# Gates and half of z as column pairs with seven products for eight, ahead of the groups

## The chip, the cores and the metric

One core of a Trainium2 chip. The metric is the device time of one execution in microseconds (us), the median of several runs.

## The reference

One step of a hybrid decoder layer on T = 1032 tokens (1024 new positions and 8 single decode tokens), width 1024, all in float32:

```python
xn = rms_norm(x)
z, xbc, dt, u, gate_a, gate_b = split(xn @ w_in)     # 2048, 4096, 32, 1024, 1024, 1024 columns
x, B, C = silu(causal_conv(xbc))                     # 8 groups: B and C of 128, x of 256 columns
y_a = rms_norm((ssd_scan(x, dt, B, C) + d * x) * silu(z))
y_b = mix(trailing means of u over 2, 4, 8, 16 positions, minus u)
merged = sigmoid(gate_a) * (y_a @ w_branch_a) + sigmoid(gate_b) * (y_b @ w_branch_b)
h = x_in + rms_norm(merged @ w_out)
out = h + rms_norm((silu(g) * up) @ w_ffn_out)       # g, up = rms_norm(h) @ w_ffn_in
```

The scan runs in chunks of 128 positions, its state carried from chunk to chunk.

## The kernel before

Values lie with 128 channels on the partitions and tokens along the row. Each float32 operand is split in two parts, a rounded high part (ACT copies) and the rest (DVE subtracts), and each product is three matmuls: high x high, high x low, low x high (`mm3`, L229). Columns of a weight come in blocks of 128; a block of the input projection reads the eight row blocks `xh[k]`, `xl[k]` in three token thirds of 344 (`in_unit`, L317): 3 x 8 x 3 = 72 matmuls. `load_w` (L172) takes weights in the order of a fixed plan, splitting one ahead, two buffers each.

The stages: input norm; pooling branch (`pool_proj`, `pool_group`, `pool_mix`, four pool groups, the mix of one beside the columns of the next); eight groups (`group_proj`, L615: conv columns B, C, x0, x1 with their four-tap conv on DVE, then two z blocks with SiLU), each beside the scan of the group before (`ssd`, L646, 18 steps, one for each token third); then 16 gate blocks (`gates`, L619) beside the last scan, with the mixer's norm and the splits of the first branch quarter at set places (L629 to L636); six branch quarters (L852), each splitting the next quarter's operands; output projection, norms, FFN in, FFN out.

FFN in (`prep`, `product`) takes a gate and an up column block against two token halves as a 2 x 2 block product with seven products for eight: weight sums and operand sums are made on DVE, each product is four row blocks x three matmuls on 258 columns, twice for the two token halves. A unit there is one column pair against 516 or 1032 tokens.

In `rp` lie 36 rows of 1060 floats, shared by all. Instructions are put in each engine's queue by a scheduler that lets an instruction go ahead of earlier code if its inputs and its buffers are there; on the chip each queue then runs in order. Two weight buffers, four banks `pj`, two `T`, one `S`, one `y` in PSUM.

## Time and profile before

| | |
|---|---|
| time, median of 3 runs | 2148.2 us (2147.57 to 2150.14) |
| the profiled execution, first to last instruction | 2146.5 us |
| busy: PE, DVE, ACT, POOL | 2091.0, 1361.0, 791.1, 406.9 us |
| moved by DMA | 243.74 MB, 114 GB/s on the mean |
| groups 2 to 5, 441 to 789 us | 348 us |
| end of the groups to the first branch quarter | 831.6 to 1032.6 us |

The profile is of one execution; no device time of its own is listed beside its span, so the span stands against the median of the runs. PE's busy time is modelled from pipelined matmuls: where PE is at its pace is read from the distance of like events. DVE, ACT and POOL times are measured, and neighbours on one engine overlap a little.

### The profile page before, as it was taken

Reading aid. Unit: us, or ns where it says so; the run is one execution under the profiler, and the core shown is the slowest. Engines: PE = TensorE matmul, PEld = TensorE weight load, DVE = VectorE, ACT = ScalarE, POOL = GpSimd, SP = SyncE. Lnnn points to the kernel's source line nnn. Section 1 sums busy time; section 2 is a strip of 40 time slices with the busy share of each in tenths; the row PEclk is TensorE's granted clock in tenths of the full one; section 3 lists DMA queues with packets and bytes.
Section 4 is the critical chain, followed back from the end, with each engine's and each line's share of the span. In section 5 each row is a group of like instructions: output and inputs, shape, how many; then the busy total and the mean of one; then the engine's idle time right before and its main releaser. Section 6 shows DMA issues by size and latency. Waiting matters only on the chain.

```text
span 2146.5 us, 36509 instructions
## 1 busy us (share of the span) xinstructions
PE 2091.0 (97%) x14722; PEld 2055.9 (96%) x14722; DVE 1361.0 (63%) x2283; ACT 791.1 (37%) x1530; POOL 406.9 (19%) x407
## 2 busy tenths in 40 slices
PE   6999999999999999999999999989999999999997
PEld 5999999999999999999999999989999999999997
DVE  7665578677787776422155775679777666654436
ACT  5443344444444444233331024445333233351112
POOL 3100234424434243210100001352000000000004
PEclk9999999999999999999999999989999999999998
DMA  3332343334434334433343444234322222252133
GB/s 126 97 112 72 100 125 125 124 105 142 139 99 127 116 128 149 137 118 136 117 150 101 145 135 151 101 101 142 96 95 90 72 78 90 99 188 69 40 101 107
DMA packets 121961, 243.74 MB, mean 114 GB/s; under 512 B 24896, under 2 KB 62912, under 8 KB 121792
## 3 DMA queue, kind: packets, MB, share of 16 engines
q1 hardware_dynamic: 121360, 241.12, 35.0%
q8 instruction: 116, 1.90, 0.4%
q14 instruction: 53, 0.43, 0.1%
q10 hardware_dynamic: 432, 0.28, 0.0%
HBM read 189.38 MB, written 51.98 MB: 112 GB/s over the span
## 4 chain that ended last, share of the span: by engine, by line
PE 71%; DVE 8%; ACT 2%; DMA 2%; issue 2%; POOL 2%; SPq 0%; DVEq 0%; ACTq 0%; POOLq 0%
PE pj L230 20%; PE pj L232 20%; PE pj L231 20%; DVE S L595 2%; DMA E<-s_ac 1%; PE y L709 1%; PE y L230 1%; PE y L231 1%; PE y L232 1%; DVE S L597 1%; PE T L230 1%; PE T L232 1%; PE T L231 1%; PE S L231 1%; PE S L232 1%
## 5 line engine op out<-in xcount | busy, mean ns | idle before, releaser
L230 PE MATMUL pj<-xh,wh 128*128 128x344 f32 x1728 | 563.3, 327 | 2.4 <-ACT xh L299 2.4
L231 PE MATMUL pj<-xl,wh 128*128 128x344 f32 x1728 | 553.0, 320 | 0.1
L232 PE MATMUL pj<-xh,wl 128*128 128x344 f32 x1728 | 552.8, 320 | 0.0
L230 PEld LDWEIGHTS pj<-xh,wh 128*128 128x128 f32 x1728 | 324.9, 188 | 14.3 <-issue 11.0
L231 PEld LDWEIGHTS pj<-xl,wh 128*128 128x128 f32 x1728 | 325.5, 188 | 1.4 <-DVE xl L300 0.8
L232 PEld LDWEIGHTS pj<-xh,wl 128*128 128x128 f32 x1728 | 325.2, 188 | 0.0
L167 DVE TENSOR_TENSOR wl<-wr,wh 128x1024 fp32r<-128x1024 f32 (+1 forms) x125 | 170.4, 1364 | 210.0 <-ACT wh L166 210.0
L166 ACT CAST wh<-wr 128x1024 fp32r<-128x1024 f32 x142 | 146.6, 1033 | 363.4 <-PE pj L231 335.5
L917 POOL TENSOR_TENSOR ssacc<-ssacc,sq 128x258 f32<-128x258 f32 (+3 forms) x41 | 43.7, 1072 | 923.8 <-ACT sq L916 917.7
L230 PE MATMUL pj<-qh,wh 128*128 128x344 f32 (+1 forms) x608 | 189.7, 312 | 0.0
L231 PE MATMUL pj<-ql,wh 128*128 128x344 f32 (+1 forms) x608 | 189.7, 312 | 0.0
L232 PE MATMUL pj<-qh,wl 128*128 128x344 f32 (+1 forms) x608 | 189.6, 312 | 0.0
L231 PE MATMUL pj<-al,wh 128*128 128x344 f32 (+2 forms) x528 | 168.9, 320 | 0.0
L232 PE MATMUL pj<-ah,wl 128*128 128x344 f32 (+2 forms) x528 | 168.8, 320 | 0.0
L230 PE MATMUL pj<-ah,wh 128*128 128x344 f32 (+2 forms) x528 | 168.8, 320 | 0.0
L683 ACT ACTIVATE E<-E,acT 128x128 f32<-128x128 f32 x256 | 83.9, 393 | 214.8 <-DMA E<-s_ac 198.1
L595 DVE SCALAR_TENSOR_TENSOR S<-U,hcw,S 128x1056 f32<-128x1056 f32 x96 | 137.3, 1430 | 3.0 <-ACT S L593 2.9
L1172 DVE TENSOR_TENSOR acc<-acc,pj 128x344 f32<-128x344 f32 (+2 forms) x120 | 60.8, 510 | 98.0 <-PE pj L232 97.9
L231 PEld LDWEIGHTS pj<-ql,wh 128*128 128x128 f32 x608 | 114.4, 188 | 0.0
L232 PEld LDWEIGHTS pj<-qh,wl 128*128 128x128 f32 x608 | 114.4, 188 | 0.0
L230 PEld LDWEIGHTS pj<-qh,wh 128*128 128x128 f32 x608 | 114.3, 188 | 0.0
L232 PEld LDWEIGHTS pj<-ah,wl 128*128 128x128 f32 x528 | 99.3, 188 | 0.0
(351 smaller groups left out, 4898.1 us busy)
## 6 DMA issues: line engine op xcount, KB each, us to landing
wr<-wi SPq DMA_DIRECT2D x72, 512.0 KB, 4.3
E<-s_ac SPq DMA_DIRECT2D x64, 256.0 KB, 4.0
wr<-wfi SPq DMA_DIRECT2D x30, 512.0 KB, 3.6
s_act<-wk SPq DMA_DIRECT2D x44, 258.0 KB, 2.0
ar<-s_act SPq DMA_DIRECT2D x22, 516.0 KB, 4.7
wu<-wfi SPq DMA_DIRECT2D x22, 512.0 KB, 3.7
wr<-wfo SPq DMA_DIRECT2D x20, 512.0 KB, 3.7
s_y<-Y SPq DMA_DIRECT2D x16, 516.0 KB, 3.8
```

The lines of the kernel that those rows point to most:

```text
L166: act.copy(out=wh, in_=raw)
L167: eng.tensor_tensor(out=wl, in0=raw, in1=wh, op=ALU.subtract)
L230: pe.matmul(out, wh, xh, start=start, stop=False)
L231: pe.matmul(out, wh, xl, start=False, stop=False)
L232: return pe.matmul(out, wl, xh, start=False, stop=stop)
L595: dve.scalar_tensor_tensor(out=S[:, :CW], in0=U[:, k:k + CW], scalar=tap(k), in1=S[:, :CW], op0=ALU.mult, op1=ALU.add)
L597: dve.scalar_tensor_tensor(out=S[:, :CW], in0=U[:, 0:CW], scalar=1.0, in1=S[:, :CW], op0=ALU.add, op1=ALU.mult)
L683: act.activation(out=E[:, h], in_=E[:, h], func=AF.Relu, scale=-1.0, bias=acT[:, c, 4 * g + h:4 * g + h + 1])
L709: pe.matmul(o, xdt[:, h, :], E[:, h, :], start=True, stop=True)
L917: eng.tensor_tensor(out=sacc[:, sl], in0=sacc[:, sl], in1=q, op=ALU.add)
L1172: dve.tensor_tensor(out=acc[ob][:, sl], in0=acc[ob][:, sl], in1=pt, op=ALU.add)
```

## The change

The input columns of both gates and of z in groups 0, 2, 4 and 6 (`ZS`) are no longer projected block by block. A new stage between the pooling branch and the groups makes them as twelve column pairs (`PAIRS`). Each pair is a 2 x 2 block product over row halves, columns and token halves with seven products for eight (`product1`): two accumulate two by two in PSUM, the rest is added on DVE at the eviction. `t_sums` makes the operand sums in the normed rows, `t_split` splits them; T1 is laid over the upper token half of `xh` and `xl` 0 to 3, whose own halves are saved to DRAM before and loaded again by `restore`. Weight sums and splits are made three items ahead (`prep1`, `RING`). A finished pair gets its tanh (z its whole SiLU) and goes to DRAM (`s_ga`, `s_gb`, `s_z`); the z rows come back at step 15 of the scan. The fourth pooling group and its mix move into this stage. PSUM is laid out anew for it and again after it.

Groups 0, 2, 4, 6 then hold four blocks, the others six. The scan beside a group takes 1.5 or 1.12 steps for each token third, and the scan of a group without z starts two steps late. The last scan runs beside the first branch quarter; that quarter's operands are loaded and split right before, the second quarter's later, and the mixer's norm moves into branch quarter 2. The split of the first quarter's weights alternates between DVE and POOL.

```diff
+H = T // 2
+ZS = (0, 2, 4, 6)
+PAIRS = "ga0 ga1 z0 ga2 z2 ga3 z4 gb0 z6 gb1 gb2 gb3".split()
+MIXES = {2: 3}
+RING = 3
+TAILS = (1, 4)
+PROD1 = ("B11", "T2", "B21", "T3", "T1", "T4", "B22")
...
-        n += 1
-        if side is not None and n % every == 0:
+def interleave(main, side, steps):
+    for n, _ in enumerate(main):
+        for _ in range(int((n + 1) * steps) - int(n * steps) if side is not None else 0):
             if next(side, StopIteration) is StopIteration:
                 side = None
+                break
     if side is not None:
         for _ in side:
             pass
...
+        for n, name in enumerate(PAIRS):
+            for i in range(2):
+                want(("pr", name, i), wi[pair_base(name) + i], raw="xp" if i else "wr")
+            if n in MIXES:
+                want(("pr", "m", MIXES[n]), wpool[MIXES[n]], 512, raw="wr")
         for g in range(G):
-            for i, blk in enumerate((WB + g, WC + g, WX + 2 * g, WX + 2 * g + 1, WZ + 2 * g, WZ + 2 * g + 1)):
+            for blk in (WB + g, WC + g, WX + 2 * g, WX + 2 * g + 1):
                 want(("in", blk), wi[blk])
-                if g == 0 and i == 2:
-                    want(("pool", 3), wpool[3], 512)
-        for base in (WGA, WGB):
-            for ob in range(KT):
-                want(("in", base + ob), wi[base + ob])
+            if g not in ZS:
+                for i in range(2):
+                    want(("in", WZ + 2 * g + i), wi[WZ + 2 * g + i])
...
+                want(("br", qi, obp), (wba if kind == "a" else wbb)[q, obp], eng=pool if qi == 0 and obp % 2 else dve)
...
+    def dbank():
+        return ps[0].tile([P, 1024], F32, name="dj", tag="dj", bufs=3)
...
+    s_b12 = dram.tile([2, 4, P, H], F32, name="s_b12")
+    lo_, hi_ = slice(0, H), slice(H, T)
+    t2 = []
+    t43 = []
+    def t_sums():
+        for k in range(4):
+            eng = pool if k % 2 else dve
+            a, b, c, d = (x_rows[i][:, sl] for i in (k, 4 + k) for sl in (lo_, hi_))
+            eng.tensor_tensor(out=d, in0=d, in1=b, op=ALU.subtract)
+            eng.tensor_tensor(out=b, in0=b, in1=a, op=ALU.subtract)
+            eng.tensor_tensor(out=a, in0=a, in1=d, op=ALU.add)
+            eng.tensor_tensor(out=c, in0=c, in1=a, op=ALU.subtract)
...
+    def t_split():
+        for k in range(4):
+            if k % 2 == 0:
+                t2.append((row(dt=F32R, name="t2h"), row(dt=F32R, name="t2l")))
+            h, l = (r_[:, k % 2 * H:k % 2 * H + H] for r_ in t2[k // 2])
+            act.copy(out=h, in_=x_rows[k][:, lo_])
+            dve.tensor_tensor(out=l, in0=x_rows[k][:, lo_], in1=h, op=ALU.subtract)
+        for k in range(4):
+            h, l = row(dt=F32R, name="t43h"), row(dt=F32R, name="t43l")
+            t43.append((h, l))
+        for sl in (hi_, lo_):
+            for k in range(4):
+                h, l = t43[k]
+                act.copy(out=h[:, sl], in_=x_rows[4 + k][:, sl])
+                dve.tensor_tensor(out=l[:, sl], in0=x_rows[4 + k][:, sl], in1=h[:, sl], op=ALU.subtract)
+            if sl is hi_:
+                t1_split()
+    def t1_split():
+        for k in range(4):
+            for i, r_ in enumerate((xh[k], xl[k])):
+                sync.dma_start(out=s_b12[i, k], in_=r_[:, hi_].bitcast(F32))
+        for k in range(4):
+            act.copy(out=xh[k][:, hi_], in_=x_rows[k][:, hi_])
+            dve.tensor_tensor(out=xl[k][:, hi_], in0=x_rows[k][:, hi_], in1=xh[k][:, hi_], op=ALU.subtract)
+    def restore():
+        for k in range(4):
+            for i, r_ in enumerate((xh[k], xl[k])):
+                sync.dma_start(out=r_[:, hi_].bitcast(F32), in_=s_b12[i, k])
+        t2.clear()
+        t43.clear()
...
+    def operand1(name, k):
+        if name == "T2":
+            return tuple(r_[:, k % 2 * H:k % 2 * H + H] for r_ in t2[k // 2])
+        if name in ("T3", "T4"):
+            return tuple(r_[:, hi_ if name == "T3" else lo_] for r_ in t43[k])
+        i = k if name in ("B11", "T1") else 4 + k
+        return tuple(r_[:, hi_ if name in ("T1", "B22") else lo_] for r_ in (xh[i], xl[i]))
...
+    def prep1(i):
+        name, pi = items1[i]
+        a_, b_ = slice(0, 512), slice(512, 1024)
+        if name == "m":
+            raw1["m"] = (load_raw("pr", "m", pi),) * 3
+        elif pi == 0:
+            g_, u_ = load_raw("pr", name, 0), load_raw("pr", name, 1)
+            s_ = xp.tile([P, T], F32, name="ws", tag="x")
+            raw1[name] = (g_, u_, s_)
+            dve.tensor_tensor(out=s_[:, a_], in0=u_[:, a_], in1=u_[:, b_], op=ALU.add)
+            dve.tensor_tensor(out=s_[:, b_], in0=s_[:, a_], in1=g_[:, a_], op=ALU.subtract)
+        g_, u_, s_ = raw1[name]
+        s_ = s_[:, :1024] if name != "m" else s_
+        if name == "m":
+            del raw1[name]
+        elif pi == 1:
+            dve.tensor_tensor(out=u_[:, a_], in0=g_[:, a_], in1=u_[:, a_], op=ALU.subtract)
+        elif pi == 2:
+            dve.tensor_tensor(out=s_[:, b_], in0=g_[:, b_], in1=s_[:, b_], op=ALU.subtract)
+        elif pi == 6:
+            del raw1[name]
+        src = g_[:, a_] if name == "m" else (g_, s_, g_, u_, s_, u_, s_)[pi][:, (a_, b_, b_, a_, a_, b_, b_)[pi]]
+        n_ = ("wh", "wl")[i % 2]
+        w = wp.tile([P, 1024], F32R, name=n_, tag=n_, bufs=2)
+        act.copy(out=w[:, a_], in_=src)
+        dve.tensor_tensor(out=w[:, b_], in0=src, in1=w[:, a_], op=ALU.subtract)
+        ring1.append(w)
...
+    def pair_rows(name):
+        if name[0] in "ux":
+            o = 16 if name[0] == "u" else 3
+            rs = [row(UW, name="U") for _ in range(2)]
+            for r_ in rs:
+                pool.memset(r_[:, 0:o], 0.0)
+        else:
+            o = 0
+            rs = [row(name="Z" if name[0] == "z" else "gt") for _ in range(2)]
+        return rs, [r_[:, o + t * H:o + t * H + H] for r_ in rs for t in range(2)]
...
+    def product1(i):
+        name, pi = items1[i]
+        if name == "m":
+            w = ring1.pop(0)
+            gi, hl = pend.pop(0)
+            assert gi == pi
+            pool_mix(gi, *hl, (w[:, 0:512], w[:, 512:1024]))
+            return
+        if pi == 0:
+            pair["rows"], pair["q"] = pair_rows(name)
+        q11, q12, q21, q22 = (two_(q_) for q_ in pair["q"])
+        w = ring1.pop(0)
+        if pi in (0, 1, 3, 4):
+            pair[pi] = dbank()
+        pt = pair[{2: 0, 5: 3, 6: 4}.get(pi, pi)]
+        first = pi in (0, 1, 3, 4)
+        for b_ in range(2):
+            cs = slice(b_ * Q, b_ * Q + Q)
+            o = pt[:, b_ * 512:b_ * 512 + Q]
+            for k in range(4):
+                h, l = operand1(PROD1[pi], k)
+                wh_, wl_ = w[:, k * P:(k + 1) * P], w[:, 512 + k * P:512 + (k + 1) * P]
+                pe.matmul(o, wh_, h[:, cs], start=first and k == 0, stop=False, skip_group_check=True)
+                pe.matmul(o, wh_, l[:, cs], start=False, stop=False, skip_group_check=True)
+                pe.matmul(o, wl_, h[:, cs], start=False, stop=k == 3, skip_group_check=True)
+        v = pt.rearrange("p (b c) -> p b c", b=2)[:, :, :Q]
+        if pi == 0:
+            act.copy(out=q22, in_=v)
+        elif pi == 1:
+            dve.tensor_tensor(out=q12, in0=q22, in1=v, op=ALU.add)
+        elif pi == 2:
+            act.copy(out=q11, in_=v)
+        elif pi == 3:
+            dve.tensor_tensor(out=q22, in0=q12, in1=v, op=ALU.add)
+        elif pi == 4:
+            dve.tensor_tensor(out=q22, in0=q22, in1=v, op=ALU.add)
+        elif pi == 5:
+            dve.tensor_tensor(out=q21, in0=q12, in1=v, op=ALU.add)
+        else:
+            dve.tensor_tensor(out=q12, in0=q12, in1=v, op=ALU.add)
...
+    def finish_pair(name, rs):
+        kind = name.rstrip("0123456789")
+        n = int(name[len(kind):])
+        if kind == "z":
+            for j in (1, 0):
+                t = row(name="tz")
+                act.activation(out=t, in_=rs[j], func=AF.Tanh, scale=0.5)
+                dve.scalar_tensor_tensor(out=rs[j], in0=t, scalar=1.0, in1=rs[j], op0=ALU.add, op1=ALU.mult)
+                sync.dma_start(out=s_z[2 * n + j], in_=rs[j])
+                yield
+        else:
+            for j in (1, 0):
+                act.activation(out=rs[j], in_=rs[j], func=AF.Tanh, scale=0.5)
+                sync.dma_start(out=(s_ga if kind == "ga" else s_gb)[2 * n + j], in_=rs[j])
...
+    t_sums()
     us = pool_proj(3)
-    pool_mix(2, *pend)
-    last_mix = pool_group(3, us)
-    # ---------------- SSD mixer ----------------
+    pool_mix(2, *pend1)
+    del pend1
+    for i in range(RING):
+        prep1(i)
+    t_split()
+    x_rows.clear()
+    pend = []
+    ps_ctx.close()
+    ps_ctx = ExitStack()
+    ps[0] = ps_ctx.enter_context(tc.tile_pool(name="ps1", bufs=2, space=PSUM))
...
+    def last_pool(us_):
+        ds_ = []
+        yield from pool_steps(3, us_, ds_)
+        dh, dl = [], []
+        for d in ds_:
+            dh.append(row(dt=F32R, name="dh"))
+            act.copy(out=dh[-1], in_=d[:, :T])
+            dl.append(row(dt=F32R, name="dl"))
+            dve.tensor_tensor(out=dl[-1], in0=d[:, :T], in1=dh[-1], op=ALU.subtract)
+            yield
+        pend.append((3, (dh, dl)))
+    def step_tail():
+        while tails and next(tails[0], StopIteration) is StopIteration:
+            tails.pop(0)
+    for i, (name, pi) in enumerate(items1):
+        if i + RING < len(items1):
+            prep1(i + RING)
+        product1(i)
+        if i == 0:
+            tails.append(last_pool(us))
+            us = None
+        if i < 13:
+            step_tail()
+        if name == "m" or pi in TAILS:
+            step_tail()
+        if name != "m" and pi == 6:
+            tails.append(finish_pair(name, pair["rows"]))
+    while tails:
+        step_tail()
+    pair.clear()
+    xp_ctx.close()
+    ps_ctx.close()
+    ps_ctx = ctx.enter_context(ExitStack())
+    ps[0] = ps_ctx.enter_context(tc.tile_pool(name="ps2", bufs=2, space=PSUM))
+    restore()
...
+            if u == 15 and g in ZS:
+                for a in range(2):
+                    d[f"z{a}"] = row(name="Z")
+                    sync.dma_start(out=d[f"z{a}"], in_=s_z[2 * g + a])
...
+    def late(g):
+        if g in ZS:
+            for _ in range(2):
+                yield
+        yield from ssd(g)
     for g in range(1, G):
-        interleave(group_proj(g), ssd(g - 1), 1)
-    interleave(gates(), ssd(G - 1), 1)
-    ssd_ctx.close()
-    # ---------------- branches, gates, merge ----------------
-    lp = ctx.enter_context(tc.tile_pool(name="lp", bufs=4))
+        interleave(group_proj(g), late(g - 1), 1.5 if g in ZS else 1.12)
+    load_quarter(0)
+    for j in range(4):
+        split_quarter(0, j)
+    lp = []
...
+            if obp == (2 if qi == 0 else 0) and qi + 1 < len(quarters):
                 load_quarter(qi + 1)
             for o2 in range(2):
                 ob = 2 * obp + o2
-                if 3 <= ob <= 6 and qi + 1 < len(quarters):
-                    split_quarter(qi + 1, ob - 3)
+                if qi == 0 and ob >= 5 or qi and 3 <= ob <= 6:
+                    if qi + 1 < len(quarters):
+                        for j in ((0,), (1,), (2, 3))[ob - 5] if qi == 0 else (ob - 3,):
+                            split_quarter(qi + 1, j)
                 if qi == 0:
                     m[ob] = row(name="m")
+                if qi == 2 and 1 <= ob <= 6:
+                    ssm_rms((ob - 1) // 2, (ob - 1) % 2)
...
+    interleave(branch(0), ssd(G - 1), 1.3)
+    ssd_ctx.close()
+    lp.append(ctx.enter_context(tc.tile_pool(name="lp", bufs=4)))
+    for qi in range(1, 6):
+        for _ in branch(qi):
+            pass
```

## Rows read from the trace of the kernel before

**Rows 1.** Page, busy time of each engine: us, share of the span, instructions.

```profile
PE 2091.0 (97%) x14722; PEld 2055.9 (96%) x14722; DVE 1361.0 (63%) x2283; ACT 791.1 (37%) x1530; POOL 406.9 (19%) x407
```

**Rows 2.** ACT timeline, gate stage: start us, length us, instruction, idle before.

```profile
998.64 1.05 ACT L166 CAST wh<-wr 128x1024 fp32r<-128x1024 f32 x1 [3.17 <-PE pj L231]
...
1032.64 1.05 ACT L166 CAST wh<-wr 128x1024 fp32r<-128x1024 f32 x1 [3.17 <-PE pj L231]
```

**Rows 3.** Timeline of DVE in the FFN-in stage.

```profile
1676.42 0.70 DVE L1129 TENSOR_TENSOR wk<-wk 128x516 f32<-128x516 f32 x1
...
1837.78 0.69 DVE L1129 TENSOR_TENSOR wk<-wk 128x516 f32<-128x516 f32 x1
```

**Rows 4.** Windows, groups: us; busy PE, PEld, DVE, ACT, POOL; clock; DMA.

```profile
441.00:789.00 348.00, 340.68 (x2310) 327.44 (x2308) 264.70 (x376) 159.26 (x351) 138.32 (x140) 1.00 0.39 124
...
441.00:471.00 30.00, 28.11 (x193) 26.91 (x193) 28.41 (x41) 16.14 (x37) 10.65 (x12) 1.00 0.32 92
...
702.00:732.00 30.00, 28.33 (x194) 27.12 (x191) 27.62 (x40) 16.75 (x37) 9.79 (x12) 1.00 0.31 92
```

**Rows 5.** DVE's instructions by line and shape, 1500 to 1850 us.

```profile
L1110 DVE TENSOR_TENSOR wk<-wk,pj 128x258 f32<-128x258 f32 x104 | 43.9, 422 | 18.7 <-PE pj L232 17.7
...
L1088 DVE TENSOR_TENSOR wl<-ws,wl 128x512 fp32r<-128x512 f32 x26 | 17.9, 687 | 1.3 <-ACT wl L1087 1.3
```

**Rows 6.** Windows of the start, the pooling stage and the FFN-in stage.

```profile
0.00:20.00 20.00, 3.21 (x12) 2.78 (x12) 11.97 (x40) 10.35 (x22) 7.89 (x16) 1.00 0.90 301
...
105.00:145.00 40.00, 40.00 (x256) 39.90 (x255) 20.73 (x28) 19.02 (x38) 4.35 (x13) 1.00 0.39 101
...
1500.00:1850.00 350.00, 350.00 (x2915) 350.00 (x2916) 253.94 (x491) 117.33 (x239) 0.00 (x0) 1.00 0.27 86
```

**Rows 7.** DVE's instructions by line and shape, 60 to 160 us.

```profile
L167 DVE TENSOR_TENSOR wl<-wr,wh 128x1024 fp32r<-128x1024 f32 x8 | 9.8, 1228 | 29.6 <-ACT wh L166 29.6
...
L384 DVE TENSOR_TENSOR S<-S 128x1024 f32<-128x1024 f32 x6 | 7.3, 1220 | 0.0
```

**Rows 8.** Timeline of SP's queue in the pooling stage.

```profile
99.41 0.34 SPq L681 DMA_DIRECT2D E<-s_ac  x1
```

**Rows 9.** DMA issues: count, KB each, median us to landing.

```profile
wr<-wi SPq DMA_DIRECT2D x72, 512.0 KB, 4.3
```

**Rows 10.** DVE's instructions by line and shape, 441 to 789 us.

```profile
L595 DVE SCALAR_TENSOR_TENSOR S<-U,hcw,S 128x1056 f32<-128x1056 f32 x48 | 70.4, 1466 | 0.2 <-ACT S L593 0.2
...
L167 DVE TENSOR_TENSOR wl<-wr,wh 128x1024 fp32r<-128x1024 f32 x24 | 39.4, 1641 | 31.4 <-ACT wh L166 31.4
...
L611 DVE SCALAR_TENSOR_TENSOR Z<-Z,pj 128x344 f32<-128x344 f32 x24 | 12.1, 506 | 30.6 <-ACT Z L610 30.6
```

**Rows 11.** Timeline where the last group ends and the gates begin.

```profile
831.62 0.45 ACT L610 ACTIVATE Z<-pj 128x344 f32<-128x344 f32 x1
...
834.18 2.89 DVE L778 TENSOR_TENSOR Y<-Y,Z 128x1032 f32<-128x1032 f32 x2 [0.45 <-POOL Y L728]
...
837.11 1.07 ACT L784 ACTIVATE q<-Y 128x1032 f32<-128x1032 f32 x1
```

**Rows 12.** Instructions by line and shape, whole span.

```profile
L813 DVE SCALAR_TENSOR_TENSOR ql<-qr,ppt,qh 128x1032 fp32r<-128x1032 f32 x16 | 20.4, 1291 | 53.5 <-ACT qh L812 53.5
...
L812 ACT ACTIVATE qh<-qr,ppt 128x1032 fp32r<-128x1032 f32 x16 | 17.7, 1151 | 0.0
```

**Rows 13.** View of the tile S: ns min/median/max, first and last start.

```profile
L595 DVE SCALAR_TENSOR_TENSOR S<-U,hcw,S x96: 1298/1309/2989, 158.5 to 811.4; 128x1056 f32<-128x1056 f32 x96
```

**Rows 14.** Timeline of a conv tap beside POOL.

```profile
499.41 2.34 POOL L749 TENSOR_TENSOR tmp<-bc,dx 128x1024 f32<-128x1024 f32 x1
...
499.92 2.95 DVE L595 SCALAR_TENSOR_TENSOR S<-U,hcw,S 128x1056 f32<-128x1056 f32 x1
```

**Rows 15.** Window of the post norms, 1405 to 1430 us.

```profile
1405.00:1430.00 25.00, 18.28 (x111) 17.53 (x110) 12.22 (x26) 14.38 (x25) 15.37 (x7) 0.73 0.14 43
```

139 lines of the change are left out of this document (70 added, 69 removed).

## The prediction

> **What bounds the kernel now.** I read the page's engine table first [rows 1]: PE is busy for 2091.0 of 2146.5 us, DVE for 1361.0. PE's busy time is modelled, so that alone isn't proof. The proof is the distance between like events. In the gate stage three column blocks of 72 matmuls take 1032.64 - 998.64 = 34.00 us [rows 2], 11.33 us a block or 157 ns a matmul of 344 columns, with nothing between them. In the FFN-in stage, which already makes seven products for eight, eight units of two token halves take 1837.78 - 1676.42 = 161.36 us [rows 3]: 20.17 us a unit of 2 x 7 x 4 x 3 = 168 matmuls, 120 ns for 258 columns. Both stages run at PE's own pace. So does almost all else: the four groups from 441 to 789 us take 348 us [rows 4], 87.0 us each, of which six blocks of 11.33 are 68.0 and the scan beside them 19.0.
>
> The same view of the groups shows where PE is not alone. In the first 30 us of a group DVE is busy 28.41 (first of the four) or 27.62 us (last; the two between are like it), 93%, and PE 28.11 or 28.33, 94.1%. Four such heads lose some 7.1 of the 7.3 us that PE lacks in the 348. So DVE at 93% costs PE about 5.9%; where it is less busy, next to nothing. This matters because the change takes work from PE in every second group and almost none from DVE.
>
> **What it removes.** 24 blocks of 72 matmuls: the 16 gate blocks and the z blocks of groups 0, 2, 4 and 6. At 11.33 us that is 271.9 us of PE [rows 2].
>
> **What it adds on PE.** Twelve column pairs of 7 products x 2 token quarters x 4 x 3 = 168 matmuls of 258 columns, the very count and shape of an FFN unit: 12 x 20.17 = 242.0 us [rows 3]. Net -29.9 us. The products accumulate two by two into one PSUM tile and are read in one instruction of 516 columns; that doesn't touch PE's pace. The scan's matmuls and the last pool mix (36 matmuls) are only moved.
>
> **Whether DVE can feed the pairs.** A pair asks DVE for 4 sums and 7 low-part subtractions of 512 columns (687 ns) and five evictions, each two of 422 ns at most [rows 5]: 11 x 0.69 + 5 x 0.84 = 11.8 us, plus some 2 x 1.3 for a z pair (a row of 1032, as in [rows 12]), against 20.17 us of PE. I take nothing for it: PE's products hide it, as they do in the FFN stage, where DVE is busy 253.9 of 350 us, 14.6 a unit, beside a PE without a gap [rows 6].
>
> **The start of the pairs** is denser. Over the first 13 products and pool mix 2 before them (13 x 2.88 + 36 x 0.157 = 43 us of PE) DVE has up to 16 operand splits of 516 columns, some 16 product splits and 8 sums of 512 (40 x 0.69 = 27.6), 9 evictions (7.6) and the last pooling group: twelve instructions of 1.22 us and small ones [rows 7], some 15.7. That is 51 us in 43. Against it, the operand sums depend only on the normed input, and the engines' order is not the code's: the first scan's load (L681) is issued at 99.41, amid the pooling stage [rows 8], long before its place in the code. So part of the splits goes into the pooling stage, where DVE is busy 20.73 of 40 us [rows 6]. Bounds 0 and 8 us; I take 2.
>
> **Two PSUM handovers** (pools closed and opened before and after the pairs): PE's next bank waits for the last eviction, a row of 0.42 to 0.84 us [rows 5]. Below by 0, above by 1 each; I take 1 for both.
>
> **Restoring the operands.** T1 lies on the upper token half of xh and xl 0 to 3, so after the last pair's fifth product eight transfers of 264 KB bring it back on SP's queue. They share it with the last gate stores, which wait for tanh. A weight block of 512 KB lands in 4.3 us [rows 9]; the fullest stretch here moves 301 GB/s [rows 6], so 2.1 MB take 7 us, landing 8 to 11 us after that product. Two more products (5.8 us) and the first third of the B block (3.8 us), which reads the untouched lower part, cover 9.6. Bounds 0 and 10 (if the queue is held); I take 2. The saves of the same halves go out during the pooling stage and hide there.
>
> **The groups.** Today's period holds 87.0 us; without the two z blocks a group is 87.0 - 22.7 = 64.3 us of PE. Its DVE work falls from 264.7 / 4 = 66.2 only by six Z products and two weight splits, 6 x 0.506 + 2 x 1.641 = 6.3 [rows 4, 10], to 59.9 us: 93%, the share at which the heads cost PE 5.9%. Of the 64.3 us 1.8 are such a loss already, so the group takes 62.5 / 0.941 = 66.4, that is +2.1. Three groups (2, 4, 6) have a scan beside them: +6. Group 0 has none and stays at PE's pace. Bounds: 0, and what it would be if DVE could not pass today's mean share of 76% (66.2 / 87): 59.9 / 0.76 = 78.8, +14.5 a group, +43. I take 6, since the stretch nearest in density sets it. In the odd groups the scan starts two steps later, which replaces the cover that the z units gave the last conv; the z loads (two of 516 KB each) have a whole half scan to land. Nothing for these.
>
> **The last scan beside the first branch quarter** costs the same PE work; DVE has at most 36 us of scan (66.2 less 12 taps, six weight splits and six Z products [rows 4, 10]) and 8.4 of splits in about 64 us (24 x 12 x 0.157 and the 19.0). What is lost is cover: the first quarter used to be split during the gates. Now its rows come free only as the last z unit ends, and at that place the scan's tail stands: DVE's Y products, behind POOL's, run from 834.18 to 837.07, ACT's squares end at 838.18, while the last z unit is read at 831.62 [rows 11]. A quarter needs four casts of 1.15 and four subtractions of 1.29 [rows 12]; the first matmul could start about 838.4, the fourth operand is there 3.9 us later, against 1.9 us of matmuls. That is some 9 us, less 2.4 us or more of the next scan's first chunk (an eighth of the 19.0), less what is done early in ACT's gaps. Bounds 1 and 10; I take 4.5. The norm's bits moved into branch quarter 2 need nothing before quarter 3.
>
> **Sum**: -29.9 + 2 + 1 + 2 + 6 + 4.5 = -14.4 on a span of 2146.5: 2132.1. The median of the runs, 2148.2, lies 1.7 above that span, so about 2134.
>
> **Rivals.** *All hidden* (0.18): the engines' order fills every gap but the handovers and a little at the branch, 4 us in all: 2148.2 - 26 = 2122. For it: PE lacks next to nothing outside the heads [rows 4].
>
> *DVE and POOL in each other's way* (0.14). A conv tap takes 1298 ns at best [rows 13] and 2.95 us when it starts 0.5 us after POOL's tmp product of 2.34 us [rows 14]. Over 441 to 789 us the taps' mean is 1466, the weight splits' 1641 against 1228 in the pooling stage [rows 7, 10]: per group 12 x 0.17 + 6 x 0.41 = 4.5 us of stretch, with POOL busy 40% (138.3 of 348) [rows 4]. The same POOL work in 64 us is 54%; stretch that grows with it is +1.6 us a group, +5 in all, on the engine that then has no slack: 2139. The Trainium skill (SBUF — State Buffer, "Who interferes with whom") says that a DVE instruction with two SBUF inputs contends with a GpSimd instruction that reads SBUF; the trace agrees, with 2.95 us for the tap beside the POOL product.
>
> *The gaps take the clock down* (0.12). From 1405 to 1430 us PE idled 6.7 us in pieces and was granted 0.73 of the clock on the mean over 25 us [rows 15], between 2.4 GHz and its lower level of 1.2: 6.8 us on top of the idling. Gaps at the three joints (pooling to pairs, pairs to groups, groups to branches) of which each cost 3 us more: 2134 + 9 = 2143.
>
> *DVE becomes the bound* (0.16), the other side: a scan step waits for DVE, PE for the scan's buffers and the weight split, at a DVE share held at 76%. Then +43 for 6: 2134 + 37 = 2171. It decides from a group of 64.3 + (29.9 - 8.5) / 3 = 71.4 us on; at 80% DVE share it is there (59.9 / 0.8 = 74.9). Against it: DVE held 93% for 30 us at a time.
>
> **How the numbers follow.** My own case has 0.40 and gives 2134, by its nearer bounds 2126 to 2142. What a measurement of this kernel can tell from no change is 0.2%, 4.3 us. Faster by more than that: 0.38 of mine, 0.18, 0.10 of the port rival, 0.05 of the clock rival: 0.71. Within: 0.02, 0.04, 0.07 and 0.02 of the DVE rival: 0.15. Slower: the rest of the DVE rival, 0.14. The range goes from below the all-hidden case, 2120, to 2152; it leaves out most of the DVE rival and a little below.
>
> **What would show each step.** Right: pairs 20.1 to 20.3 us apart; groups 2, 4 and 6 between 64 and 69 us with DVE above 88%; odd groups near 87; PE gaps of 1 to 6 us at the joint of group 7 and the branches and under 3 us at the other two; branch quarter 0 near 64 us. Wrong: pairs beyond 21 us (DVE or PSUM holds them); a first pair over 26; group periods over 71 us with PE waiting for DVE; granted clock below 0.9 in the 10 us behind a joint; matmuls of B in group 0 that wait for the restore.

## The result, and where the profile after has the time

The changed kernel takes 2166.2 us (median of 4 runs, 2162.9 to 2169.3); the kernel before, beside it, 2149.2 (4 runs, 2147.6 to 2150.7). The ratio is 1.0078, 95% interval 1.0062 to 1.0093: slower by 17 us, where 2134 was forecast. The profiled execution, the longest of the four, has a span of 2167.5 us.

The first view is the page's engine table with the granted clock of the core beside it, after and then (second clock row) before.

```profile
PE 2079.9 (96%) x15010; PEld 2040.5 (94%) x15010; DVE 1486.8 (69%) x2461; ACT 824.7 (38%) x1576; POOL 401.6 (19%) x413
```

```profile
core 0: 2167.5 us, clock 0.983
```

```profile
core 0: 2146.5 us, clock 0.993
```

Against [rows 1]: 29.9 us of work were taken from PE on paper, but its busy time fell by 11.1 us alone: 18.8 are missing. The mean granted clock went from 0.993 to 0.983, and one hundredth of 2167 us is 21.7, which also counts time in which PE idled at the lower clock. And PE's idle time rose from 2146.5 - 2091.0 = 55.5 to 2167.5 - 2079.9 = 87.6 us, by 32.1. Idle +32.1, busy -11.1: the 21 us between the two spans. So the work did leave PE, and waits and a lower clock ate more than that.

Next, where. The landmarks are PE's own instructions: the first matmul after pool mix 2, the end of the last product of a pair, the last projection matmul of the groups, the last branch matmul (1324.5 after, 1306.0 before). All in us from the profiled executions.

| stretch | on paper | forecast | after | lost against the forecast |
|---|---|---|---|---|
| start to the first matmul behind pool mix 2 | 144.3 (before) | 144.3 | 154.2 | 9.9 |
| twelve pairs and pool mix 3 | 12 x 20.17 + 5.7 = 247.7 | 250.2 | 253.8 | 3.6 |
| groups 0 to 7 | 45.3 + 3 x 64.3 + 4 x 87.0 = 586.2 | 594.7 | 605.1 | 10.4 |
| last scan and branches | 19.0 + 273.2 = 292.2 | 296.7 | 311.4 | 14.7 |
| the rest | 840.5 (before) | 840.5 | 843.0 | 2.5 |

The stretches of the forecast add up to 2126.4; its 2132.1 also kept the 5.7 us that the kernel before has over its own work in the gates and groups. So 41.1 - 5.7 = 35.4 us are to be explained.

**The pairs.** The stores of the z pairs, in SP's timeline, are two pairs apart:

```profile
276.13 2.07 SPq L730 DMA_DIRECT2D s_z<-Z  x2
316.41 2.07 SPq L730 DMA_DIRECT2D s_z<-Z  x2
356.69 2.07 SPq L730 DMA_DIRECT2D s_z<-Z  x2
```

That is 40.28 us, 20.14 a pair, as in [rows 3]. The next windows show the joint into the pairs, the ten us behind PE's wait at their start, the pairs, an even and an odd group, and the joint behind group 7 (busy PE, PEld, DVE, ACT, POOL; clock; DMA):

```profile
145.00:160.00 15.00, 11.68 (x79) 11.20 (x77) 8.81 (x15) 12.19 (x24) 0.67 (x3) 1.00 0.47 151
161.00:171.00 10.00, 9.16 (x63) 8.95 (x64) 10.00 (x16) 3.93 (x8) 0.00 (x0) 0.83 0.19 60
160.00:400.00 240.00, 238.16 (x1963) 237.94 (x1964) 150.39 (x219) 91.15 (x139) 0.10 (x1) 0.99 0.32 103
545.00:610.00 65.00, 62.83 (x437) 59.59 (x437) 58.88 (x84) 33.62 (x75) 29.11 (x36) 1.00 0.46 151
610.00:705.00 95.00, 89.55 (x588) 85.68 (x587) 70.70 (x98) 42.71 (x94) 34.98 (x35) 0.96 0.39 125
1013.00:1045.00 32.00, 21.77 (x128) 18.16 (x127) 22.17 (x32) 16.29 (x36) 14.40 (x9) 0.79 0.65 209
```

The wait is in PE's timeline (first line below): at the start of the pairs PE stands 3.84 us until a split weight is there. The other two lines are the first convolution taps of groups 2 and 3, in DVE's timeline:

```profile
161.19 0.39 PE L690 MATMUL dj<-t2h,wl 128*128 128x258 f32 x1 [3.84 <-ACT wl L642]
```

```profile
556.24 4.03 DVE L715 SCALAR_TENSOR_TENSOR S<-U,hcw,S 128x1056 f32<-128x1056 f32 x3 [0.62 <-ACT S L713]
622.32 1.30 DVE L715 SCALAR_TENSOR_TENSOR S<-U,hcw,S 128x1056 f32<-128x1056 f32 x1
```

The taps are 66.1 us apart, those of groups 4 and 5, and of 6 and 7, 66.5; behind the odd groups 1, 3 and 5 it is 87.7, 93.5 and 89.3. PE is full in the pairs and nearly so in the even group, where DVE is at 58.88 / 65 = 91%. The odd group behind it, with DVE at 74%, is the one that lacks 5.5 us of PE and is granted 0.96. The last window lacks 10.2 us of PE at 0.79.

**The odd groups.** PE's waits from 455 to 1013 us (total, times, longest), and its timeline where group 3 begins:

```profile
PE T L897 <- DVE S L717: 10.4, 3, 3.7
PE S L931 <- DVE eA L947: 9.1, 7, 2.1
```

```profile
621.30 0.33 PE L897 MATMUL T<-ident,S 128*128 128x128 f32 x1 [3.67 <-DVE S L717]
621.61 0.40 PE L251 MATMUL pj<-xh,wh 128*128 128x344 f32 x1
621.85 0.32 PE L252 MATMUL pj<-xl,wh 128*128 128x344 f32 x1
...
624.24 0.49 PE L251 MATMUL pj<-xh,wh 128*128 128x344 f32 x1
624.52 0.49 PE L252 MATMUL pj<-xl,wh 128*128 128x344 f32 x1
```

L897 transposes the x block of the even group for its scan's first chunk; L717 is the last operation of that block's convolution. In an even group nothing is projected behind that block any more, so the transpose reaches the head of PE's queue before the convolution ends, and the next group's projections, ready as they are, stand behind it. The Trainium skill (TensorE: Matmul & The Clock Gate, "Step-by-step: what each phase is for") says that matmuls stay in program order and only weight loads are pulled ahead; the trace agrees, with 3.67 us in which PE ran none of them. Behind the wait the projections are 0.28 us apart instead of 0.16, at the lower of the two clock levels (1.2 for 2.4 GHz): the granted clock of these ten us is 0.83. The windows are those of the first, the second (3.03 us, to 781.25) and the third wait, and one behind a wait of 1.78 us at 662.31:

```profile
620.00:630.00 10.00, 8.70 (x46) 8.70 (x47) 8.89 (x10) 3.42 (x7) 2.10 (x4) 0.83 0.19 55
781.00:791.00 10.00, 9.75 (x65) 9.74 (x66) 8.61 (x13) 3.18 (x6) 1.59 (x4) 1.00 0.17 55
930.00:940.00 10.00, 6.31 (x34) 6.01 (x33) 8.85 (x7) 5.24 (x10) 7.88 (x7) 0.84 0.29 77
662.00:672.00 10.00, 9.69 (x57) 9.21 (x58) 7.68 (x16) 7.21 (x18) 3.19 (x5) 0.83 0.26 82
```

So two of the three waits were followed by the lower clock and the second, of 3.03 us, was not; behind the shorter one, with PE busy for 5.53 of the seven us before it, the clock did fall. The length of a single wait doesn't tell which it will be.

**The pooling stage.** POOL's, DVE's, ACT's and PE's timelines, one fence each:

```profile
67.37 0.19 POOL L393 COPY pv<-U 128x8 f32<-128x8 f32 x1
68.78 3.54 POOL L568 TENSOR_TENSOR xrow<-xrow 128x516 f32<-128x516 f32 x2
```

```profile
67.59 0.17 DVE L411 TENSOR_REDUCE ss<-pv 128x8 f32<-128x16 f32 x1 [1.33 <-POOL pv L393]
69.82 1.26 DVE L412 COPY S<-ss 128x8 f32<-128x8 f32 x1
71.07 1.80 DVE L566 TENSOR_TENSOR xrow<-xrow 128x516 f32<-128x516 f32 x1
73.93 0.23 DVE L417 TENSOR_TENSOR S<-S,U 128x1 f32<-128x1 f32 x1
```

```profile
74.25 1.05 ACT L431 CAST dh<-S 128x1032 fp32r<-128x1032 f32 x1 [7.98 <-POOL U L353]
78.78 1.47 ACT L360 COPY U<-pj 128x344 f32<-128x344 f32 x4
```

```profile
79.26 0.66 PE L251 MATMUL pj<-xh,wh 128*128 128x344 f32 x1 [5.22 <-ACT U L360]
```

The operand sums (L565 to L568) were hoisted into the pooling stage. Beside POOL's, a DVE copy of eight columns takes 1.26 us (0.16 before, the same step) and a sum of 516 columns up to 1.80 (0.69 alone). And the copy `pv` on POOL (L393), which the chain on DVE reads, stands behind POOL's sums in POOL's queue and runs at 67.37. The split of a pooling row waits for that DVE chain, the PSUM evictions stand behind the split in ACT's queue, and PE runs out of PSUM banks for 5.2 us, with the clock at 0.83 in the ten us after. The Trainium skill (SBUF — State Buffer, "Who interferes with whom") has DVE instructions with two SBUF inputs contend with GpSimd's reads; the 1.80 us agree.

**The joint behind group 7.** SP's timeline, then DVE's, then two windows:

```profile
1009.45 5.52 SPq L909 DMA_DIRECT2D E<-s_ac  x2
1015.06 0.38 SPq L1007 DMA_DIRECT2D o_ssmp<-hT  x1
...
1022.12 1.46 SPq L1011 DMA_DIRECT2D s_y<-Y  x2
1023.63 2.45 SPq L1030 DMA_DIRECT2D qr<-s_y  x4
```

```profile
1020.36 2.88 DVE L1010 TENSOR_TENSOR Y<-Y,Z 128x1032 f32<-128x1032 f32 x2 [1.47 <-POOL Y L956]
...
1034.33 6.90 DVE L1045 SCALAR_TENSOR_TENSOR ql<-qr,ppt,qh 128x1032 fp32r<-128x1032 f32 x4
```

```profile
1000.00:1020.00 20.00, 16.34 (x114) 15.15 (x112) 10.32 (x21) 6.84 (x20) 8.24 (x7) 0.97 0.49 163
1020.00:1040.00 20.00, 14.70 (x78) 11.93 (x78) 17.75 (x24) 9.10 (x16) 11.55 (x8) 0.69 0.93 303
```

Quarter 0 is rows of groups 0 and 1, long since in DRAM. Yet its four loads leave SP at 1023.63, behind the store of group 6's Y, which waits for the end of a scan that runs past its group. The splits start at 1032.6, the first branch matmul at 1034.36, 21.2 us after the last projection matmul ends (1013.1); the loads take 5.3 to 9.2 us to land, in a stretch that moves 303 GB/s. In the kernel before the last projection matmul ends at 1032.8 and the first branch matmul starts at 1032.59, without a gap.

### The profile page after: what moved, and what is told of

It reads as the page before. It is cut to its first block, busy times and chain, and to the rows that moved or that the text cites. A ratio compares the mean times of both kernels' runs of the same rounds, so it can differ in the third digit from the quotient of the medians.

```text
span 2167.5 us, 37539 instructions
## 1 busy us (share of the span) xinstructions
PE 2079.9 (96%) x15010; PEld 2040.5 (94%) x15010; DVE 1486.8 (69%) x2461; ACT 824.7 (38%) x1576; POOL 401.6 (19%) x413
## 4 chain that ended last, share of the span: by engine, by line
PE 78%; DVE 12%; DMA 3%; issue 2%; POOL 2%; ACT 2%; SPq 0%; ACTq 0%; DVEq 0%; POOLq 0%
PE pj L251 18%; PE pj L252 18%; PE pj L253 18%; PE dj L692 4%; PE dj L690 4%; PE dj L691 4%; DVE S L715 2%; DVE S L717 1%; PE y L937 1%; DMA E<-s_ac 1%; DMA bc<-s_bc 1%; DVE wl L188 1%; PE y L251 1%; PE y L252 1%; PE y L253 1%
## 5 line engine op out<-in xcount | busy, mean ns | idle before, releaser
L251 PE MATMUL pj<-xh,wh 128*128 128x344 f32 x1152 | 379.6, 332 | 8.4 <-ACT U L360 5.2
L252 PE MATMUL pj<-xl,wh 128*128 128x344 f32 x1152 | 373.8, 325 | 0.1
L253 PE MATMUL pj<-xh,wl 128*128 128x344 f32 x1152 | 372.2, 323 | 0.0
L187 ACT CAST wh<-wr 128x1024 fp32r<-128x1024 f32 (+1 forms) x117 | 120.9, 1034 | 361.6 <-PE pj L252 329.9
L251 PEld LDWEIGHTS pj<-xh,wh 128*128 128x128 f32 x1152 | 219.8, 192 | 17.9 <-issue 9.1
L252 PEld LDWEIGHTS pj<-xl,wh 128*128 128x128 f32 x1152 | 220.6, 191 | 1.5 <-DVE xrow L318 0.6
L253 PEld LDWEIGHTS pj<-xh,wl 128*128 128x128 f32 x1152 | 220.6, 191 | 0.0
L188 DVE TENSOR_TENSOR wl<-wr,wh 128x1024 fp32r<-128x1024 f32 (+1 forms) x102 | 137.3, 1347 | 96.3 <-ACT wh L187 85.8
L715 DVE SCALAR_TENSOR_TENSOR S<-U,hcw,S 128x1056 f32<-128x1056 f32 x96 | 127.5, 1328 | 7.9 <-ACT S L713 7.1
L252 PEld LDWEIGHTS pj<-al,wh 128*128 128x128 f32 x528 | 99.4, 188 | 0.0
```

Of the source, the lines that this page charges most:

```text
L187: act.copy(out=wh, in_=raw)
L188: eng.tensor_tensor(out=wl, in0=raw, in1=wh, op=ALU.subtract)
L251: pe.matmul(out, wh, xh, start=start, stop=False)
L252: pe.matmul(out, wh, xl, start=False, stop=False)
L253: return pe.matmul(out, wl, xh, start=False, stop=stop)
L715: dve.scalar_tensor_tensor(out=S[:, :CW], in0=U[:, k:k + CW], scalar=tap(k), in1=S[:, :CW], op0=ALU.mult, op1=ALU.add)
```

## The experiments

The stages of the runs, from the same landmarks (us; the column of the groups ends with the last projection matmul and so holds any gate blocks behind group 7; for e9_joint, which has no pairs, it starts at the first matmul behind pool mix 2, at 145.7; medians are of timed runs, the stages of one profiled execution each):

| run | median | ratio to before | first product | pairs | groups (and gate blocks) | then to the branches' end | rest |
|---|---|---|---|---|---|---|---|
| after | 2166.2 | 1.0078 | 154.2 | 253.8 | 605.1 | 311.4 | 843.0 |
| e1_gap | 2166.0 | 1.0079 | 152.3 | 233.1 | 646.6 | 298.0 | 836.1 |
| e2_dve | 2163.1 | 1.0066 | 147.3 | 253.6 | 608.4 | 310.3 | 841.6 |
| e2_late | 2157.5 | 1.0042 | 145.8 | 254.5 | 608.9 | 307.7 | 837.7 |
| e3_noz | 2157.8 | 1.0043 | 154.3 | 173.1 | 682.6 | 307.8 | 838.1 |
| e5_old | 2165.1 | 1.0071 | 145.5 | 214.3 | 676.3 | 283.4 | 834.6 |
| e6_all | 2153.4 | 1.0025 | 145.3 | 133.5 | 747.3 | 284.7 | 839.1 |
| e7_late | 2139.5 | 0.9955 | 145.1 | 254.0 | 592.1 | 308.9 | 839.5 |
| e9_joint | 2154.9 | 1.0025 | - | - | 870.3 | 298.3 | 841.7 |
| e10_best | 2133.3 | 0.9923 | 145.6 | 214.1 | 655.3 | 278.6 | 836.1 |
| e11_gap | 2136.2 | 0.9941 | 145.2 | 234.1 | 620.8 | 298.0 | 835.8 |
| e12_late | 2143.3 | 0.9971 | 153.1 | 253.1 | 589.7 | 308.9 | 838.7 |
| e13_ev | 2147.9 | 0.9993 | 145.2 | 133.5 | 747.6 | 278.2 | 838.9 |
| e14_rate | 2165.7 | 1.0083 | 153.3 | 253.3 | 615.4 | 303.2 | 838.6 |
| e15_lag | 2141.4 | 0.9969 | 152.7 | 253.3 | 588.3 | 308.0 | 836.8 |

The last column, which no edit touches, moves by 8 us between profiled executions; a single profile's total is not to be read finer than that. "After" is profiled in the longest of its executions, e15_lag in the shortest of seven, e5_old in the shortest of six.

### The scan's start beside odd groups: e15_lag, e14_rate, e12_late, e7_late

```diff
-            for _ in range(2):          # late(g): steps before the scan starts
+            for _ in range(4):          # e15_lag, e12_late, e7_late
-        interleave(group_proj(g), late(g - 1), 1.5 if g in ZS else 1.12)
+        interleave(group_proj(g), late(g - 1), 1.5 if g in ZS else 1.25)   # e14_rate, e12_late, e7_late
```

e7_late stands on e2_late, the others on the changed kernel. e7_late and e12_late came first:

> On the kernel with the late operand sums (2157.5 us), the scan of an even group starts four units late beside the odd group, not two, and goes at 1.25 steps a unit, not 1.12. Theory A, the waits of the scan's first transposes for the last convolution of the even group (10.4 us in three waits) are what the odd groups lose: 2149 to 2152. Rival B, the DVE work of the two is the bound there, and the later scan only pushes the same wait to its end and into the next group: 2156 to 2161.

> The changed kernel with one edit: the scan of an even group starts four units late beside the odd group and goes at 1.25 steps a unit (two units and 1.12 in the changed kernel). Operand sums and joint as in the changed kernel. Theory A, the groups lose to the scan's first transposes, which wait at the head of the matmul queue for the last convolution, and to the lower granted clock behind each such wait, 18 us as measured beside the late sums: 2148 us (2145 to 2152). Rival B, only the waits themselves, 9 to 10 us, belong to this, and the rest came from the two edits together: 2155 to 2159.

e7_late: 2139.5, 18 us under e2_late and better than either theory; e12_late: 2143.3, 23 under the changed kernel and a little under theory A's range. Two numbers differ, so they were parted:

> The changed kernel with one number changed: the scan beside an odd group goes at 1.25 steps a unit for 1.12; it still starts two steps late. Theory A, the start decides (the first transposes wait for the last convolution of the even group): no gain, 2162 to 2170, and the wait of the first transposes is there in the odd groups as before, some 10 us in three. Rival B, the rate decides (at 1.12 the scan runs past its group's end and into the next): 2143 to 2152.

> The changed kernel with one number changed: the scan of an even group starts four steps late beside the odd group, not two; the rate stays at 1.12 steps a unit. Theory A, the start decides: 2143 to 2150, as with both numbers changed (2143.3 us). Rival B, the rate decides: 2160 to 2170, the scan now runs still further past its group's end.

The rate alone: 2165.7, no gain in all, and the wait is there as before (first fence, PE's waits of e14_rate); it only moves time, 10 us more in the groups and 8 less behind them. The start alone: 2141.4, interval of the ratio 0.9957 to 0.9980, all of the gain; among PE's waits of e15_lag (second fence) that of L897 is gone, and windows like those above have the full clock (third):

```profile
PE T L897 <- DVE S L717: 11.3, 3, 4.3
```

```profile
PE y L937 <- DVE Y L952: 9.0, 7, 1.5
PE S L931 <- DVE eA L947: 5.4, 5, 1.9
PE T L895 <- ACT bcr L884: 1.0, 1, 1.0
```

```profile
620.00:640.00 20.00, 20.00 (x135) 19.41 (x134) 15.94 (x19) 8.02 (x15) 3.65 (x9) 1.00 0.23 64
925.00:945.00 20.00, 20.00 (x135) 19.41 (x134) 15.99 (x19) 8.18 (x15) 4.00 (x9) 1.00 0.26 65
```

The groups take 588.3 us for 586.2 on paper. The windows over all groups, of the changed kernel and of e15_lag:

```profile
408.00:1013.10 605.10, 580.39 (x3911) 556.32 (x3911) 473.46 (x649) 285.07 (x618) 224.75 (x252) 0.99 0.41 132
```

```profile
406.00:994.30 588.30, 571.92 (x3896) 549.98 (x3897) 478.21 (x647) 287.41 (x615) 219.28 (x251) 1.00 0.43 136
```

PE's idle time falls from 24.7 to 16.4 us, by less than the 10.4 of the three waits, as the waits at L937 grow from 3.3 to 9.0. Its busy time falls by 8.5 for the same work (15 matmuls are missing on record, at most 2.4 us of it): that is the clock. One number, two steps more, turns the change from 0.8% slower to 0.3% faster.

### Groups of one kind: e3_noz

```diff
-ZS = (0, 2, 4, 6)
-PAIRS = "ga0 ga1 z0 ga2 z2 ga3 z4 gb0 z6 gb1 gb2 gb3".split()
+ZS = ()
+PAIRS = "ga0 ga1 ga2 ga3 gb0 gb1 gb2 gb3".split()
-        interleave(group_proj(g), late(g - 1), 1.5 if g in ZS else 1.12)
+        interleave(group_proj(g), late(g - 1), 1)
```

> Only the gate columns are pairs: the four z pairs are taken out, every group projects its own z again (six units), and the scan of the group before runs beside each group at one step a unit, as in the kernel before. On paper: four pairs of 20.17 us removed, four times 22.7 us of z units added, +9.9 us. Theory A, the groups lost 18.6 us over the sum of their work because groups of 12 and of 18 units follow each other and the scan and the convolutions meet on DVE: all groups run at the 87 us of the groups in the kernel before, the loss goes, and the time is about 2158 (2154 to 2163). Rival B, the groups are slower for another reason that stays (restored operands, buffers): 2172 to 2178.

2157.8: theory A's time, by another reason than its own. Four pairs (80.7 us) were exchanged for 90.7 us of blocks, and it still gained 8.4, since with z blocks behind the last convolution no transpose waits for it (L897 is not among PE's waits there; theory A blamed DVE, but e15_lag loses the waits while DVE's busy time in the groups rises from 473.5 to 478.2): the groups take 682.6 for 45.3 + 22.7 + 7 x 87.0 = 677.

### The operand sums: e2_dve, e2_late

```diff
-            eng = pool if k % 2 else dve
+            eng = dve                                # both
-    t_sums()
     us = pool_proj(3)
     pool_mix(2, *pend1)
+    with tc.issue_after(last_dl[0].ins):             # e2_late: behind pooling group 2's last split on DVE
+        t_sums()
```

> The sixteen operand sums of the token quarters all go to DVE, in the same place; before, eight of them were POOL's. Theory A, POOL's two-operand sums stretched the small DVE operations that the pooling chain waits for: the first product of the pairs starts 5 to 9 us earlier (145 to 149 us for 154) and the time is 2157 to 2161. Rival B, what hurts is where the sums stand, ahead of the pooling rows on DVE: with sixteen instead of eight of them there, some 10 us of DVE work in one place, the stage is as long or longer, 2164 to 2170.

> The sixteen operand sums all go to DVE and behind the split of the third pooling group, so that nothing of the pooling chain up to there is queued behind them. Theory A (POOL's stretch) gives what the same sums on DVE in their old place give, 2157 to 2161; rival B (their place) gives that only here: 2157 to 2161 here and no gain there. A third way: the sums now end so late that the first products of the pairs wait for their splits, and what the pooling stage gains is lost at the first product: 2164 to 2168.

The engine alone brings the first product from 154.2 to 147.3, the place another 1.5: 6.9 of 8.4 us belong to POOL's share of the sums. That isn't all stretch, as theory A has it: in e2_dve POOL's copy `pv` runs at 58.00 for 67.37, and DVE's reduction of it (L411) at 61.75 for 67.59, 5.8 us earlier, by POOL's queue; the rest of the chain, up to its last subtraction (L417), is 3.1 us shorter without POOL's sums beside it.

```profile
58.00 0.20 POOL L393 COPY pv<-U 128x8 f32<-128x8 f32 x1
```

By the times alone the theories are not parted: e2_dve's 2163.1 lies between their ranges, and its runs (2161.5 to 2164.8) overlap those of the changed kernel. The medians gain 3.1 and 8.7, with groups that took 3 to 4 us more in both profiles. In e2_late the stage has no hole:

```profile
60.00:80.00 20.00, 20.00 (x129) 20.00 (x128) 14.70 (x28) 4.23 (x9) 1.37 (x7) 1.00 0.35 77
```

The two edits don't add in full: beside the later scan (e12_late to e7_late) the sums bring 3.8 us.

### The joint: e9_joint, e1_gap, e11_gap

e9_joint is the kernel before with this part and what hangs on it (the mixer's norm in branch quarter 2, the second quarter loaded and split later):

```diff
-    interleave(gates(), ssd(G - 1), 1)
-    ssd_ctx.close()
+    interleave(gates(), None, 1)
...
+    interleave(branch(0), ssd(G - 1), 1)
+    ssd_ctx.close()
```

> The kernel before with one part of the change alone: the last scan runs beside the first branch quarter (one step a unit), and the 48 gate units run without a scan beside them; quarter 0 is loaded and split under the last gate units, as before. The work is the same. Theory A, the scan beside a branch quarter costs nothing by itself when the quarter's rows are there: 2147 to 2153. Rival B, it costs by itself, because the branch's own loads, the next quarter's splits and the scan's loads meet: 2156 to 2168.

2154.9, ratio 1.0012 to 1.0038 in the interval: between the two. The branches with the scan take 298.3 for 292.2, 6 us over the work, although quarter 0 is there. That is what the scan's place costs with the moves that hang on it; the changed kernel lost 19.2 there.

e1_gap (on the changed kernel) and e11_gap (on e7_late) put two plain gate blocks ahead of the branch:

```diff
-PAIRS = "... gb1 gb2 gb3".split()
+PAIRS = "... gb1 gb2".split()
-    load_quarter(0)
-    for j in range(4):
-        split_quarter(0, j)
+    def lead():                      # gb blocks 6 and 7, units n = 1..6
+        ...
+                if n == 1:
+                    load_quarter(0)
+                elif n >= 3:
+                    split_quarter(0, n - 3)
-    interleave(branch(0), ssd(G - 1), 1.3)
+    interleave(lead(), ssd(G - 1), 1.3)        # e1_gap: lead goes on with branch(0)
+    interleave(lead(), None, 1)                # e11_gap
+    interleave(branch(0), ssd(G - 1), 1.3)     # e11_gap
```

> The last pair of gate columns (gb3) is projected again as two plain gate blocks, after group 7 and ahead of the first branch quarter; quarter 0's four rows are loaded at their first unit and split at the units behind it; the last scan runs beside these six units and then beside the branch. On paper that costs 2 x 11.33 - 20.17 = +2.5 us. Theory A, the joint behind group 7 lost 19.3 us over the sum of its work because quarter 0's rows were loaded and split with no matmuls left to cover them: the hole between group 7 and the first branch matmul goes under 4 us, and the time falls by about 13 us, to 2153 (2149 to 2157). Rival B, the last scan is slow beside a branch quarter whatever is loaded when: the stretch from group 7's end to the end of branch quarter 5 keeps its excess and the time is 2165 to 2171.

> Late operand sums and the scan four units late (2139.5 us together); gb3 as two plain gate blocks after group 7 with no scan beside them, quarter 0 loaded and split under these six units, and then the last scan beside the first branch quarter as in the changed kernel. On paper +2.5 us. Theory A, of the 17 us that the joint loses here only the 5 to 6 remain that the last scan beside a branch quarter cost the kernel before: 2139.5 + 2.5 - 11 = 2131 us (2128 to 2135). Rival B, with the scan's loads behind quarter 0's in one queue the hole only moves to the scan: 2138 to 2143.

e1_gap gained nothing in all, 2166.0, but not as rival B has it: from the last projection matmul to the branches' end it takes 298.0 for 311.4, and the hole ahead of the first branch matmul is gone (0.3 us; 4.6 us of waits for the splits stand behind it). What took it back is mainly its groups: from the first convolution tap of group 1 to the last of group 7 they take 536.3 us against 524.8, though every engine has the same order of instructions there; see the last section. e11_gap takes the same 298.0 and gains 3.3 of the 8.5 expected, between its two theories; its two blocks and the joint before them cost 28.7 us instead of 22.7.

### The joint as it was, and the best version: e5_old, e6_all, e13_ev, e10_best

```diff
-PAIRS = "... gb1 gb2 gb3".split()
+PAIRS = "... gb1".split()            # gb blocks 4 to 7 plain, after group 7
-    interleave(branch(0), ssd(G - 1), 1.3)
+    interleave(last_gates(), ssd(G - 1), 1.5)   # load_quarter(0) at unit 4, splits at units 9 to 12
+    for qi in range(6):                         # branches without a scan
+        for _ in branch(qi):
+            pass
...
-                    ssm_rms((ob - 1) // 2, (ob - 1) % 2)
+                    with tc.issue_after(last_mm[0].ins):        # e13_ev, e10_best
+                        ssm_rms((ob - 1) // 2, (ob - 1) % 2)
```

All four load and split the second quarter where the kernel before does, and have the late sums of e2_late; e6_all and e13_ev are without z pairs, e10_best has the later scan.

> On the kernel with the late operand sums (2157.5 us), gb2 and gb3 are projected as four plain gate blocks after group 7, the last scan runs beside these twelve units at 1.5 steps a unit, and quarter 0 is loaded at the fourth of them and split at the last four: the joint of the kernel before. On paper +5.0 us (4 x 11.33 - 2 x 20.17). Theory A, the joint of the changed kernel lost 19 us over its work, by quarter 0's late load and the last scan's own loads in one queue: most of it goes, 2145 us (2141 to 2150). Rival B, as with one plain pair the loads and the scan collide beside the gates as well and only the 5 us are added: 2157 to 2163.

> All three places mended at once: sums late on DVE, no z pairs (every group with its own z, scan at one step a unit), gb2 and gb3 as plain blocks beside the last scan; six gate pairs are left. Theory A, the three losses are separate places and add: 2157.5 + 5.0 - 17 (joint) - 8.4 (groups, as measured) = 2137 us (2132 to 2143), faster than both kernels. Rival B, the losses overlap and the joint gives no more once the groups are even: 2144 to 2150.

Theory A failed both times, and rival B's range too: 2165.1 (six runs, spread from 2155.8 to 2173.9) and 2153.4. e5_old still starts the scan two steps late and has the three waits of the transposes, 3.5 to 4.2 us each. The branches of the two, now without a scan, still took 283 to 285 us for 273.2. PE's timeline and a window of e6_all, then the same window of e13_ev, in which the matmuls of the sums of squares (L260) are held back to the place that the program gives them:

```profile
1038.05 1.24 PE L260 MATMUL T<-ones,ssacc 128*128 128x1 f32 x6 [2.73 <-POOL ssacc L1022]
```

```profile
1040.00:1050.00 10.00, 10.00 (x49) 10.00 (x50) 1.88 (x5) 4.32 (x8) 0.00 (x0) 0.74 0.42 155
```

```profile
1040.00:1050.00 10.00, 10.00 (x65) 10.00 (x64) 3.81 (x3) 4.94 (x9) 0.00 (x0) 1.00 0.52 198
```

> The kernel with all three places mended and even groups (2153.4 us) with one further edit: the matmuls of the last sums of squares are held behind a branch unit of the third quarter. Theory A, their wait for the last sum (2.7 us) at the head of the first branch quarter, 0.7 us behind it and the granted clock after it (0.87 for 20 us) cost 6 us: 2147 us (2144 to 2150). Rival B, that wait covers another one: 2151 to 2156.

2147.9, as theory A has it; the stretch takes 278.2 for 284.7. Of these 6.5 us 3.4 are waits (2.7, and 0.7 behind it); 49 matmuls instead of 65 in ten us are 16 x 0.157 = 2.5 us for the clock.

> Late operand sums on DVE, the scan four units late beside odd groups (together 2139.5 us measured), and the joint as in the kernel before: gb2 and gb3 as four plain gate blocks beside the last scan, quarter 0 loaded and split under them. New: the matmuls of the sums of squares are held behind a branch unit of the third quarter, where the program names them; in the two runs with plain gate blocks beside the last scan they stood at the head of the first branch quarter and waited there for the last sum, 2.7 us and the clock behind it. Theory A, the joint's 17 us over its work were the late loads and that wait: 2139.5 + 5.0 - 17 = 2128 us (2124 to 2133). Rival B, the hand-over to the branches costs its 10 us by something else: 2135 to 2141.

2133.3, ratio 0.9923 (0.9910 to 0.9935): faster than both kernels, than the changed one by 33 us; between its two theories, at the upper end of A's. Its joint is down to 278.6 us after the last projection matmul; its page has PE busy for 2066.0 us, 25.0 less than before for 29.9 - 5.0 = 24.9 on paper, and idle for 2129.7 - 2066.0 = 63.7, at a mean clock of 0.994.

```profile
PE 2066.0 (97%) x14962; PEld 2028.8 (95%) x14962; DVE 1476.3 (69%) x2441; ACT 822.1 (39%) x1570; POOL 392.3 (18%) x405
```

## Why the prediction was wrong, by its steps

- **Removed and added work, -29.9 us: right.** Pairs 20.14 us apart, and in e10_best, at the clock of the kernel before, PE's busy time fell by what paper says.
- **DVE feeding the pairs: right.** 150.39 of 240 us beside a full PE.
- **Even groups, +2.1 each: right.** The taps put them at 66.1 to 66.5 us for 66.4 forecast, with DVE at 91%; in e15_lag all groups together are 2 us over paper, as two of the odd ones take less than 87.0. The DVE rival needed groups beyond 71.4 us and is out, and the port rival with it: e7_late's taps take 1482 ns on the mean, e2_late's 1327, and e7_late's groups are 16.8 us shorter. That the DVE rival's 2171 lies near the measured 2166 is chance.
- **"Nothing for these", the odd groups: the step that failed most.** I said that two steps of delay replace the cover of the z units for the last convolution. They don't; four do. The waits (10.4 us in three) and the lower clock behind them cost 16.8 us in the groups' stretch (605.1 to 588.3). The median fell by 25 and the profiled span by 28.4; of the latter the joint gave 3.4 and the other 8.2 lie in stages that the edit doesn't touch.
- **Nothing for the operand sums: failed.** I read from [rows 8] that they may move into the pooling stage and counted it as a help to the pairs. There they stood in a chain that ACT and PE wait for, in POOL's queue ahead of its copy and on DVE beside POOL's sums: 8.4 us, of which 6.9 by POOL's share.
- **+4.5 for the joint: far too low**, 19.2. I counted the splits behind the last z unit, and no load at all: four rows behind a store that waits for the scan before, and that scan ending late. Of the 19.2 some 6 belong to the scan beside a branch and what moved with it (e9_joint). The other 13 went with the hole that the plain blocks closed, but in e11_gap 6 us came back in those blocks, so what the late load costs is shown only to lie between 7 and 13.
- **The clock rival, 0.12: the right mechanism, not all of the places.** It priced three joints at 3 us each (its 6.8 us from [rows 15] also count the 6.7 us in which PE idled). Two of them show it: 0.83 from 161 to 171 us at the start of the pairs, 0.69 from 1020 to 1040. So do the pooling stage (0.83) and the odd groups, behind two of their three waits at L897, which it didn't name.
- **The start of the pairs, the handovers and the restore, 5 us: about right.** The pair stretch is 6.1 over paper, with the wait of 3.84 us at its start and the lower clock behind it, which the estimate didn't have; the restore shows in no wait.

Still open: what the 6 us of e9_joint are made of, the 6 us that the two blocks of e11_gap cost over their work, and why the clock falls behind some waits and not behind others.

## What to carry to other kernels

An instruction that waits at the head of an in-order queue costs what stands behind it, not what it needs: when work is taken out of a stage, ask which filler stood between a producer and the consumer on the full engine, and move the consumer by as much. Price a wait on a full TensorE at more than its length, for the clock that may be lower behind it: here three waits of 10.4 us in all went with 16.8, waits of 3.4 with 6.5. A load that moves to a new place in the queue is late by all that waits ahead of it there, however old its data are.
